# A spare tile of 160 bytes instead of 32 at the high end of SBUF: where the two halves of the buffers stand modulo 2048 bytes

## The chip, the cores and the metric

The kernel runs on one NeuronCore of one Trainium2 chip. The metric is the device time of one execution, in microseconds (us). Five engines work side by side and meet at semaphores: TensorE (PE; its weight loads are listed apart as PEld), VectorE (DVE), ScalarE (ACT), GpSimd (POOL), and SyncE (SP), which issues most of the DMA transfers. A matmul on PE has two operands in SBUF, the core's on-chip memory of 128 partitions: the stationary one (128 columns, loaded by a weight load just before) and the moving one (up to 512 columns, streamed through). The result goes to PSUM.

## The reference

One layer of an encoder on x of shape 1 x 1024 x 1024 in float32: a SwiGLU half step, a mixer of attention (4 query heads, 2 key heads of 128) and a bidirectional gated recurrence (4 heads of 128), a second SwiGLU half step with an inner width of 2816, and a last norm.

```
def swiglu_half_step(x, gain, w_in, w_out):
    h = rms_norm(x, gain)
    gate, up = jnp.split(h @ w_in, 2, axis=-1)
    return (jax.nn.silu(gate) * up) @ w_out
...
x = x + 0.5 * swiglu_half_step(x, ffn1_norm[l], ffn1_w_in[l], ffn1_w_out[l])
x = x + hybrid_mixer(x, l, ...)
x = x + 0.5 * swiglu_half_step(x, ffn2_norm[l], ffn2_w_in[l], ffn2_w_out[l])
x = rms_norm(x, final_norm[l])
```

## The kernel before

**Numbers.** Almost every product runs in three matmuls on operands that are split into a high and a low part (`split`, L103 and L104: ACT copies the high part, DVE subtracts it from the source). So one product of 128 rows is (high, high), (high, low), (low, high).

**Stages.** The kernel goes through five stages, each with pools of buffers of its own.

- `ffn_up`, for both half steps. The first two of the 22 column blocks are computed plainly (`plain`, L277, 256 columns at a time); the other 20 by a scheme of seven half-size products (`product`, L294, 512 columns). `unit` does seven `product` calls for one column block, and each is 4 blocks of k times 3 matmuls. The stationary operand is a weight tile from the pool `wop` (`hl_in_ffn`), the moving one a tile of the pools `B` or `T` (`ffn_B`, `ffn_T`).
- `ffn_down`, for both half steps: L402, 512 columns; stationary `hl_act_ffn` (pool `ah`), moving `hl_out_ffn` (pool `wo`).
- The mixer's projections: `proj_T` (L167, 512 columns; stationary `hl_rec_w`, moving `hm`) and `natural` (L495, 256 columns; stationary `hm`, moving the weights), and between them the recurrence.
- Attention: scores `s` (L798, 512 columns, stationary `qT`, moving `kT`), values `pv` (L830, 256 columns), and the output projection `project` (L855, 512 columns), which is called for the recurrence (`py`, stationary `recT`, moving `hl_wor`) and for the attention (`pa`, stationary `oT`, moving `hl_woa`).

The profile writes a matmul as out<-moving,stationary.

**Order.** The framework schedules the instructions when the program is built, and derives the waits from which tiles share memory. Loads stand in SP's queue in that order.

**Addresses.** A pool with `side="right"` takes its memory from the high end of SBUF downwards, the others from the low end upwards. All buffers named below are multiples of 2048 bytes apart within their side (small tiles of statistics and some of the recurrence are not), so each side has one residue modulo 2048. On the right the first tile is the spare one, `align` (L55), which no instruction reads or writes. The places in the built program, in bytes from the start of a partition:

| tiles | side | starts at | modulo 2048 |
|---|---|---|---|
| `hl_in_ffn` (wop) | left | 55104, then every 4096 | 1856 |
| `hl_out_ffn` (wo), `hl_act_ffn` (ah) | left | 44864 and 73536, then every 4096 | 1856 |
| `qT`, `recT` | left | 55104, 38720 | 1856 |
| `ffn_T`, `ffn_B` | right | 114624 and 163776, then every 16384 | 1984 |
| `hm`, `kT`, `v_attn`, `pT` | right | 163776, then every 16384 | 1984 |
| `hl_rec_w`, `hl_ri_w`, `hl_wor`, `hl_woa` (w2, the last of four in wo) | right | 139200, then every 8192; 90048 | 1984 |
| `oT` | right | 98240, 106432 | 1984 |

Inside a tile a matmul's operand starts at a multiple of 512 bytes, a moving one of 512 columns at a multiple of 2048. So a matmul has a relation of its own between its two operands: both left, both right, or one on each side, and in the last case the two starts differ by 128 bytes more than a multiple of 512. Both left: L402. Both right: L167, L495, L830 and `pa` of L855. One on each side: L277, L294, L798 and `py` of L855.

Of the kernel before, what the change touches and what calls it, by code (L numbers as in the profile page):

```python
# [12 lines left out]
F32 = mybir.dt.float32  # L13
# [8 lines left out]
P = 128  # L22
# [22 lines left out]
class Trunk:  # L45
    def __init__(self, ctx, tc, io):
        self.tc, self.nc, self.io = tc, tc.nc, io
        nc = self.nc
        pool = lambda name, **kw: ctx.enter_context(tc.tile_pool(name=name, **kw))
        self.const = pool("const", bufs=1)  # L50
        self.gpool = pool("gains", bufs=1)
        self.stat = pool("stat", bufs=4)
        self.dpool = pool("scratch", bufs=1, space=bass.MemoryType.DRAM)
        self.ident = self.const.tile([P, P], F32, name="ident")
        pool("align", bufs=1, side="right").tile([P, 8], F32, name="align")  # L55
        make_identity(nc, self.ident)
        self.banks = {}

# [1097 lines left out]
```

## Time and profile before

| what | us |
|---|---|
| median of 3 runs | 2138.0 (2133.77 to 2138.9) |
| the profiled execution | 2136.09 |
| its span, first to last instruction | 2134.3 |
| PE busy | 2053.5 (96%) |
| DVE, ACT, POOL busy | 1160.3, 780.2, 390.5 |

The profiled execution's own time stands 1.8 us above its span. Matmuls are pipelined: one is listed with about 390 ns, but the next starts long before its end. How fast they go is read from their number in a stretch in which PE doesn't stop, or from the starts of two groups. A list of a stretch counts every matmul that has any part in it.

### The profile page before, as it was taken

The page shows a single profiled execution, that of the slowest core. Times are in us where ns is not written, and L with a number is a line of the kernel's source. Part 1 is how long each engine was busy: PE and PEld are TensorE (multiplying, and loading weights), DVE is VectorE, ACT ScalarE, POOL GpSimd, SP SyncE. Part 2 cuts the span into 40 slices and gives each one's busy share as a digit, 9 for nine tenths or more (in the row PEclk, how much of TensorE's full clock was granted, in tenths as well). Part 3 has the DMA queues.
Part 4 walks back from the last instruction along what each step waited for, and adds up shares of the span by engine and source line. Part 5 has one row for each costly group of instructions (what it writes and reads, how often), then busy time and mean ns, then how long its engine had stood idle before and what let it go on. Part 6 is the DMA issues. An engine that isn't in the chain of part 4 may idle for free.

```text
span 2134.3 us, 27958 instructions
## 1 busy us (share of the span) xinstructions
PE 2053.5 (96%) x10849; PEld 1755.2 (82%) x10849; DVE 1160.3 (54%) x1951; ACT 780.2 (37%) x1295; POOL 390.5 (18%) x278
## 2 busy tenths in 40 slices
PE   5899999999999899999998999988999999999998
PEld 5888888887888798989998888878888888878886
DVE  6555554535363516788872567654645554443634
ACT  4333333324343313333332546533333333333432
POOL 2333232210000000121120323312422222100000
PEclk9999999999999999999999999999999999999999
DMA  5422322117464211121234522363322221264542
GB/s 167 124 80 80 93 89 74 60 70 260 142 223 148 74 45 43 32 80 40 80 100 148 175 92 81 108 192 105 98 84 79 75 89 55 74 236 142 185 148 79
DMA packets 208124, 232.12 MB, mean 109 GB/s; under 512 B 9444, under 2 KB 169464, under 8 KB 207992
## 3 DMA queue, kind: packets, MB, share of 16 engines
q1 hardware_dynamic: 205688, 221.95, 32.9%
q0 software_dynamic: 2304, 8.39, 1.0%
q8 instruction: 85, 1.39, 0.3%
q14 instruction: 47, 0.39, 0.1%
HBM read 175.78 MB, written 54.53 MB: 108 GB/s over the span
## 4 chain that ended last, share of the span: by engine, by line
PE 90%; DVE 5%; ACT 2%; DMA 1%; issue 1%; POOL 0%; SPq 0%; DVEq 0%; ACTq 0%; POOLq 0%
PE py_ffn L402 22%; PE pa_ffn L294 16%; PE pd_ffn L294 10%; PE rec_ps L167 6%; PE pc_ffn L294 5%; PE pb_ffn L294 5%; PE pp_ffn L277 4%; PE ri_ps L495 2%; PE rg_ps L495 2%; PE lv L561 2%; PE s L798 2%; PE py L855 2%; PE pv L830 2%; PE pa L855 2%; PE aq_ps L495 1%
## 5 line engine op out<-in xcount | busy, mean ns | idle before, releaser
L402 PE MATMUL py_ffn<-hl_out_ffn,hl_act_ffn 128*128 128x512 f32 x2112 | 482.4, 390 | 4.0 <-ACT hl_out_ffn L103 3.4
L402 PEld LDWEIGHTS py_ffn<-hl_out_ffn,hl_act_ffn 128*128 128x128 f32 x2112 | 397.0, 188 | 88.6 <-ACT hl_out_ffn L103 5.0
L104 DVE TENSOR_TENSOR hl_out_ffn<-raw_out_ffn,hl_out_ffn 128x512 fp32r<-128x512 f32 x176 | 120.1, 688 | 235.1 <-ACT hl_out_ffn L103 234.9
L294 PE MATMUL pa_ffn<-ffn_T,hl_in_ffn_S 128*128 128x512 f32 x960 | 242.4, 395 | 0.0
L294 PEld LDWEIGHTS pa_ffn<-ffn_T,hl_in_ffn_S 128*128 128x128 f32 x960 | 180.8, 188 | 42.1
L103 ACT CAST hl_out_ffn<-raw_out_ffn 128x512 fp32r<-128x512 f32 x176 | 107.8, 620 | 266.1 <-PE py_ffn L402 258.4
L104 DVE TENSOR_TENSOR hl_in_ffn_S<-s_ffn,hl_in_ffn_S 128x512 fp32r<-128x512 f32 x160 | 163.6, 1026 | 29.4 <-ACT hl_in_ffn_S L103 29.4
L103 ACT CAST hl_in_ffn_S<-s_ffn 128x512 fp32r<-128x512 f32 x160 | 99.1, 621 | 201.3 <-PE pd_ffn L294 175.2
L104 DVE TENSOR_TENSOR hl_in_ffn_A<-raw_in_ffn,hl_in_ffn_A 128x512 fp32r<-128x512 f32 x128 | 103.5, 813 | 125.7 <-ACT hl_in_ffn_A L103 125.7
L103 ACT CAST hl_in_ffn_A<-raw_in_ffn 128x512 fp32r<-128x512 f32 x136 | 83.7, 623 | 182.2 <-PE pc_ffn L294 77.8
L167 PE MATMUL rec_ps<-hm,hl_rec_w 128*128 128x512 f32 x576 | 134.7, 392 | 0.0
L167 PEld LDWEIGHTS rec_ps<-hm,hl_rec_w 128*128 128x128 f32 x576 | 107.1, 188 | 21.6
L294 PE MATMUL pd_ffn<-ffn_T,hl_in_ffn_S 128*128 128x512 f32 x480 | 124.6, 395 | 0.0
L294 PE MATMUL pb_ffn<-ffn_B,hl_in_ffn_A 128*128 128x512 f32 x480 | 124.2, 395 | 0.0
L294 PE MATMUL pa_ffn<-ffn_B,hl_in_ffn_A 128*128 128x512 f32 x480 | 119.4, 398 | 0.0
L294 PE MATMUL pc_ffn<-ffn_T,hl_in_ffn_A 128*128 128x512 f32 x480 | 118.0, 394 | 0.0
L294 PE MATMUL pd_ffn<-ffn_B,hl_in_ffn_S 128*128 128x512 f32 x456 | 112.1, 394 | 0.0
L294 PEld LDWEIGHTS pa_ffn<-ffn_B,hl_in_ffn_A 128*128 128x128 f32 x480 | 91.2, 191 | 21.1
L294 PEld LDWEIGHTS pb_ffn<-ffn_B,hl_in_ffn_A 128*128 128x128 f32 x480 | 90.5, 189 | 21.2
L294 PEld LDWEIGHTS pd_ffn<-ffn_T,hl_in_ffn_S 128*128 128x128 f32 x480 | 90.5, 188 | 21.2
L277 PE MATMUL pp_ffn<-ffn_B,hl_in_ffn_A 128*128 128x256 f32 x768 | 101.1, 294 | 6.9 <-DVE ffn_B L186 3.9
L294 PEld LDWEIGHTS pc_ffn<-ffn_T,hl_in_ffn_A 128*128 128x128 f32 x480 | 90.4, 188 | 21.1
(245 smaller groups left out, 3123.7 us busy)
## 6 DMA issues: line engine op xcount, KB each, us to landing
raw_in_ffn<-in_ffn_w_in SPq DMA_DIRECT2D x88, 512.0 KB, 4.2
raw_out_ffn<-in_ffn_w_out SPq DMA_DIRECT2D x88, 512.0 KB, 3.8
raw_act_ffn<-d_act SPq DMA_DIRECT2D x88, 256.0 KB, 4.0
d_act<-g_ffn SPq DMA_DIRECT2D x80, 256.0 KB, 2.2
x<-d_x SPq DMA_DIRECT2D x24, 512.0 KB, 4.9
x<-in_x SPq DMA_DIRECT2D x16, 512.0 KB, 5.3
d_x<-x SPq DMA_DIRECT2D x16, 512.0 KB, 2.8
raw_rec_w<-in_w_in_mix SPq DMA_DIRECT2D x12, 512.0 KB, 4.0
```

What stands on the lines that cost most here:

```text
L103: nc.scalar.copy(hl[:, 0, :], src)
L104: (lo_engine or nc.vector).tensor_sub(hl[:, 1, :], src, hl[:, 0, :].bitcast(F32))
L167: nc.tensor.matmul(out, hl[:, a, ks], h[half][b][:, k, cols], start=(k == 0 and i == 0), stop=(k == NK - 1 and i == 2),)
L277: nc.tensor.matmul(ps[j][:, odd * 256 : (odd + 1) * 256], A[2 * j + k // 4][:, a, ks], B[k // 4][:, b, k % 4, cols], start=(k == 0 and i = ...
L294: nc.tensor.matmul(ps, A[:, a, ks], T[key][:, b, k, :], start=(first and k == 0 and i == 0), stop=(k == 3 and i == 2), skip_group_check=True,)
L402: nc.tensor.matmul(py[d], ah[:, a, o : o + P], wo[d][:, b, :], start=(f == 0 and i == 0), stop=(f == NF - 1 and i == 2),)
L495: nc.tensor.matmul(ps[:, tt, :], h[half][a][:, k, ts], hl[k // 4][:, b, ws], start=(k == 0 and i == 0), stop=(k == NK - 1 and i == 2),)
L561: nc.tensor.matmul(pl[:, cs], now[:, 0, cs], now[:, 1, cs], start=True, stop=True)
L798: nc.tensor.matmul(ps[:, ks], qT[:, a, qs], kT[:, b, kv, ks], start=(i == 0), stop=(i == 2))
L830: nc.tensor.matmul(ps, vt[:, j, a, vs], pT[j][:, b, i4, :], start=(st == 0 and i == 0), stop=(st == NT - 1 and i == 2),)
L855: nc.tensor.matmul(py, lhs(a, n), units[n][:, b, ds], start=(n == 0 and i == 0), stop=(n == 3 and i == 2),)
```

## The change

```
-        pool("align", bufs=1, side="right").tile([P, 8], F32, name="align")
+        pool("align", bufs=1, side="right").tile([P, 40], F32, name="align")
```

The spare tile takes 40 floats instead of 8, so every buffer of the right side moves down by 128 bytes: residue 1856 in place of 1984. Nothing on the left moves. `ffn_T` then begins at 114496, the byte at which the topmost left buffer of that stage ends. The order of the instructions is the same on all five engines. What changes beside the addresses is two waits, one added and one moved, because other pieces of memory now overlap.

On POOL, at the start of the second half step's `ffn_up` (the sums of L221 to L223; `x_7` and `xn_` are the last rows of attention, being stored; in brackets stand the semaphores waited for, by engine or DMA queue; `t_ffn_0` are the sums of the first row pair):

```order
 L910 DMA d_xn_78<-xn_n_6_11700 128x1024 [waits DMASW5_49,DVE_49]
 L904 DMA d_x_77<-x_7_11715 128x1024 [waits DMAHW7_49,DMASW6_49,DVE_49]
-L223 TENSOR_TENSOR t_ffn_0_12108<-t_ffn_0_12106,xn_0_11801 128x512 [waits DMAHW4_49,DVE_49]
+L223 TENSOR_TENSOR t_ffn_0_12108<-t_ffn_0_12106,xn_0_11801 128x512 [waits DMAHW4_49,DVE_49,PE_49]
 L910 DMA d_xn_78<-xn_n_7_11746 128x1024 [waits DMASW7_49,DVE_49]
 L221 TENSOR_TENSOR t_ffn_1_12172<-xn_3_11839 128x512 [waits DMAHW0_49,PE_49,Pool_49]
```

The first sum that L223 makes there now waits for PE as well: for the last `pa` matmul of attention, since its buffer now overlaps the place of `oT`.

On SP, in the second half step's `ffn_down` (L1094 loads the rows of x; DMASW are the transfers that POOL issued, those of L904 among them):

```order
 L385 DMA raw_act_ffn_7_0_15659<-d_act_102 128x2x256 [waits DMAHW5_49,DVE_49]
 L1094 DMA x_0_15477<-d_x_77 128x1024 [waits Pool_49]
-L1094 DMA x_1_15479<-d_x_77 128x1024 [waits DMASW6_49,DMAHW6_49,DMASW4_49,PE_49]
-L1094 DMA x_2_15481<-d_x_77 128x1024 [waits DMAHW7_49]
+L1094 DMA x_1_15479<-d_x_77 128x1024 [waits DMAHW6_49,DMASW6_49,PE_49]
+L1094 DMA x_2_15481<-d_x_77 128x1024 [waits DMAHW7_49,DMASW4_49]
 L1094 DMA x_3_15483<-d_x_77 128x1024 [waits DMAHW2_49,DMAHW0_49]
 L383 DMA raw_out_ffn_7_0_15657<-in_ffn_w_out 128x1024 [waits DMAHW1_49,DVE_49]
```

One wait for a transfer of POOL's goes from the second load to the third.

## Rows read from the trace of the kernel before

**Rows 1.** The page: busy time of each engine (share of the span) and number of instructions; the chain of work that ended last, by engine and by line.

```profile
PE 2053.5 (96%) x10849; PEld 1755.2 (82%) x10849; DVE 1160.3 (54%) x1951; ACT 780.2 (37%) x1295; POOL 390.5 (18%) x278
...
PE 90%; DVE 5%; ACT 2%; DMA 1%; issue 1%; POOL 0%; SPq 0%; DVEq 0%; ACTq 0%; POOLq 0%
PE py_ffn L402 22%; PE pa_ffn L294 16%; PE pd_ffn L294 10%; PE rec_ps L167 6%; PE pc_ffn L294 5%; PE pb_ffn L294 5%; PE pp_ffn L277 4%; PE ri_ps L495 2%; PE rg_ps L495 2%; PE lv L561 2%; PE s L798 2%; PE py L855 2%; PE pv L830 2%; PE pa L855 2%; PE aq_ps L495 1%
```

**Rows 2.** Matmuls in three stretches that hold nothing but L294: stretch, its length, PE's busy time and number of matmuls, granted clock of PE, DMA share, GB/s.

```profile
100.00:280.00 180.00, 180.00 (x776) 1.00 0.29 85
290.00:480.00 190.00, 190.00 (x819) 1.00 0.22 71
1500.00:1870.00 370.00, 370.00 (x1594) 1.00 0.25 77
```

**Rows 3.** The same view for two stretches of L402 alone, and for two of L167 alone (the last two lines).

```profile
500.00:720.00 220.00, 220.00 (x972) 1.00 0.55 177
1890.00:2110.00 220.00, 220.00 (x972) 1.00 0.53 173
...
796.00:832.00 36.00, 36.00 (x160) 1.00 0.20 59
1026.00:1046.00 20.00, 20.00 (x90) 1.00 0.42 132
```

**Rows 4.** The instructions of single lines: number, shortest, median and longest duration in ns as the profile lists it, first and last start in us, shapes. L294, L402, L167, L855 and L798 in turn.

```profile
L294 PE MATMUL pa_ffn<-ffn_T,hl_in_ffn_S x960: 390/393/404, 107.3 to 1880.1; 128*128 128x512 f32 x192
...
L294 PE MATMUL pa_ffn<-ffn_B,hl_in_ffn_A x480: 390/392/776, 97.2 to 1857.8; 128*128 128x512 f32 x160
...
L294 PE MATMUL pb_ffn<-ffn_B,hl_in_ffn_A x480: 390/393/404, 100.5 to 1863.4; 128*128 128x512 f32 x160
...
L294 PE MATMUL pc_ffn<-ffn_T,hl_in_ffn_A x480: 390/393/404, 103.3 to 1866.1; 128*128 128x512 f32 x160
...
L294 PE MATMUL pd_ffn<-ffn_T,hl_in_ffn_S x480: 390/393/404, 106.1 to 1874.5; 128*128 128x512 f32 x160
...
L294 PE MATMUL pd_ffn<-ffn_B,hl_in_ffn_S x456: 390/392/404, 124.7 to 1870.8; 128*128 128x512 f32 x152
...
L294 PE MATMUL pe_ffn<-ffn_B,hl_in_ffn_S x24: 390/393/404, 482.9 to 1877.3; 128*128 128x512 f32 x24
...
L402 PE MATMUL py_ffn<-hl_out_ffn,hl_act_ffn x2112: 387/389/761, 490.4 to 2123.4; 128*128 128x512 f32 x192
...
L167 PE MATMUL rec_ps<-hm,hl_rec_w x576: 387/389/481, 794.6 to 1046.6; 128*128 128x512 f32 x192
...
L855 PE MATMUL py<-hl_wor,recT x192: 389/393/689, 1176.3 to 1262.0; 128*128 128x512 f32 x192
...
L855 PE MATMUL pa<-hl_woa,oT x192: 387/389/497, 1270.8 to 1407.8; 128*128 128x512 f32 x192
...
L798 PE MATMUL s<-kT,qT x192: 387/395/628, 1167.8 to 1372.4; 128*128 128x512 f32 x192
```

**Rows 5.** PE in order of time, in attention: start in us, time from the first start to the last end, engine, line, operation, tiles, shapes, number.

```profile
1244.16 5.75 PE L855 MATMUL py<-hl_wor,recT 128*128 128x512 f32 x24
1249.76 0.51 PE L830 MATMUL pv<-pT,v_attn 128*128 128x256 f32 x3
...
1330.32 2.99 PE L855 MATMUL pa<-hl_woa,oT 128*128 128x512 f32 x12
1333.14 0.60 PE L817 MATMUL ptp<-ident,p 128*128 128x128 f32 x4
...
1396.99 11.19 PE L855 MATMUL pa<-hl_woa,oT 128*128 128x512 f32 x48
```

**Rows 6.** The view of rows 2 for matmuls of 256 columns: a stretch of L277 and one of L495.

```profile
30.00:52.00 22.00, 22.00 (x188) 1.00 0.28 93
1104.00:1160.00 56.00, 56.00 (x469) 1.00 0.45 146
```

**Rows 7.** All engines in a stretch of `ffn_up` and in the two parts of attention (busy time and number for PE, PEld, DVE, ACT, POOL, then granted clock, DMA share, GB/s); and one group of L294 in the view by line (busy time, mean ns of one, idle time of PE before them).

```profile
290.00:480.00 190.00, 190.00 (x819) 154.03 (x819) 89.75 (x127) 64.57 (x112) 45.29 (x33) 1.00 0.22 71
...
1176.00:1262.00 86.00, 84.68 (x465) 71.66 (x464) 48.03 (x70) 39.73 (x69) 27.14 (x20) 1.00 0.43 145
1270.00:1408.00 138.00, 128.31 (x784) 111.42 (x783) 98.28 (x231) 77.90 (x145) 45.49 (x42) 1.00 0.33 107
...
L294 PE MATMUL pa_ffn<-ffn_T,hl_in_ffn_S 128*128 128x512 f32 x960 | 242.4, 395 | 0.0
```

**Rows 8.** The places of the two waits: POOL in order of time (start, duration, and in brackets the idle time before and who ended it); then L904 on POOL with its transfers' time to landing, and L1094 on SP's queue, in the view of rows 4.

```profile
1413.57 1.64 POOL L223 TENSOR_TENSOR t_ffn<-t_ffn,xn 128x512 f32<-128x512 f32 x1 [2.59 <-DVE t_ffn L222]
...
L904 POOL DMA_DIRECT2D d_x<-x x8: 533/604/762, 1281.1 to 1410.4; - x8
...
DMA to landing us min/median/max: 3.0/4.1/5.7
...
L1094 SPq DMA_DIRECT2D x<-d_x x8: 319/430/1242, 1893.6 to 1902.5; - x8
```

## The prediction

> **What bounds the kernel now.** I read the page first: busy times and the chain of work that ended last [rows 1]. PE is busy 96% of the span and makes up 90% of that chain, so a change that touches no instruction can only matter by how fast PE's matmuls follow each other. L294 and L402 are the two big lines of the chain: the four L294 entries together hold 36%, L402 holds 22%. Next I took stretches that hold one line only and counted matmuls [rows 2, 3]. A list counts every matmul with any part in the stretch, and one lasts some 0.39 us [rows 4], so the spacing is (length + 0.39 us) / number.
>
> - L294: 180.39 / 776, 190.39 / 819 and 370.39 / 1594 all give 232.4 ns [rows 2].
> - L402: 220.39 / 972 gives 226.7 ns, twice [rows 3].
> - L167: 36.39 / 160 and 20.39 / 90 give 227.4 and 226.6 ns [rows 3].
>
> All three are matmuls of 128 by 512 with 128 stationary columns, at a granted clock of 1.00, the 2.4 GHz level, with PE never idle in the stretch. L402 keeps its 226.7 with DMA at a share of 0.55, L294 is slower at 0.22 to 0.29, so transfers aren't the reason. What goes with the difference is the sides of the operands. L402 has both on the left, L167 both on the right, L294 one on each. L167's moving tile `hm` stands at the very addresses of `ffn_B`, and L402's stationary tiles have the residue of L294's, so it is neither operand alone.
>
> The durations say it again, and inside one stage [rows 4]. With both operands on one side (L402, L167, `pa`) shortest and median are 387 and 389 ns each time. With one on each side L294 has 390 and 392 or 393, `py` 389 and 393, `s` a median of 395. `py` and `pa` are the same line and the same loop, in the same stage; only the tiles differ. The spacings of attention agree: 24 `py` matmuls from 1244.16 to the next group at 1249.76 are 233.3 ns each; 48 `pa` matmuls, 11.19 us less one duration over 47, are 229.8 [rows 5].
>
> **The change, part by part.**
>
> *L294.* After it both operands have residue 1856, the relation that L402 has today. Its matmuls number 960 + 4 x 480 + 456 + 24 = 3360 [rows 4]. PE is idle for 0.0 us before them [rows 7], so their spacing is the stage's time. If it goes from 232.4 to 226.7, the gain is 5.7 ns x 3360 = 19.1 us. The trace has no matmul of L294 at equal residue, so I bound the new spacing: 226.6, the fastest row at equal residue, gives 19.5 us; 235, the slowest (12 `pa` matmuls from 1330.32 to 1333.14 [rows 5], between short pieces of other work), gives a loss of 8.7 us. I take 226.7, because L294 runs without a break as L402 does, which is the nearest row; that slow `pa` piece follows a switch of kind. What is late next: in the 190 us of [rows 7] DVE is busy for 89.75, ACT 64.57, POOL 45.29, at a DMA share of 0.22. PE needs 2.5% less time; none of them comes near.
>
> *`py` and `s`.* 192 each [rows 4], with one operand on each side. Their stretches are short, so I take from them not L402's spacing but what `pa` reaches: 233.3 - 229.8 = 3.5 ns x 384 = 1.3 us. PE is busy 84.68 of 86 us and 128.31 of 138 in these parts [rows 7], so most of it is on the path: 1.0 us. Bounds: 0, if the waits between pieces take it, and 384 x 6.6 ns (233.3 down to 226.7) = 2.5 us.
>
> *L277.* 256 columns, operands on both sides; the wide matmuls' penalty is not there. With 0.29 us for one, 22.29 / 188 = 118.6 ns against 56.29 / 469 = 120.0 for L495, whose operands have equal residue [rows 6]. If L277 takes L495's spacing, its 768 matmuls lose 1.1 us. It stands half beside waits for its operands early in both stages, so I count a loss of 0.5 us; bounds 0 and 1.1.
>
> *L830, L495, L167, `pa`, L402.* Both operands move together or neither does: nothing.
>
> *The two waits.* L223 now also waits for the last `pa` matmul. That ends at 1396.99 + 11.19 = 1408.18 [rows 5], L223 starts at 1413.57 after it waited for DVE [rows 8]: met 5.4 us earlier. Behind it in POOL's queue stand the last store of xn and L221, neither later than now. On SP, the transfers of L904 are issued by 1410.4 and land within 5.7 us, the loads of L1094 begin at 1893.6 [rows 8]: met by 480 us. Both cost nothing. The cover would be gone only if attention ended 5.4 us later against L223, and it doesn't.
>
> *The spare tile.* No instruction touches it: nothing.
>
> Sum: -19.1 - 1.0 + 0.5 = -19.6 us. The profiled execution took 2136.09, its span 2134.3; that gives 2116.5. The median of the runs, 2138.0, stands 1.9 us above the profiled one and the fastest run 2.3 below it. I split the difference and say 2117.
>
> **A rule that speaks against it.** L402 and L294 differ by 5.7 ns a matmul [rows 2, 3]. The Trainium skill, page "TensorE: Matmul & The Clock Gate", section "Part 2: What happens when you issue a matmul", says that TensorE reads the stationary and the moving operand through two independent ports, so that loading weights doesn't take bandwidth from a running matmul; "SBUF — State Buffer", section "SBUF: two separate sides", says that TensorE never waits for anyone there. By these two the addresses couldn't matter and the time would stay at 2136 to 2138. The trace doesn't agree: `py` and `pa` differ in nothing but where their tiles stand.
>
> **The rivals.**
>
> 1. *The residues aren't the cause, and nothing changes: 2137.* Then L294 would be slowed by what works beside it, such as POOL, busy 45.29 us there [rows 7] and not at all in `ffn_down`. Against it: POOL is busy in both parts of attention too, 27.14 of 86 us where `py` runs and 45.49 of 138 where `pa` runs [rows 7], and `pa` has the fast median. For it: no row shows a right and a left operand at equal residue. This holds the case that the distance, and not the residue, decides. The two rules above end here.
> 2. *Half the gain: 2126.* Equal residue lets the matmuls run fast only after some undisturbed ones, and in L294 the product, the moving tile and the PSUM bank change every 12. The spacing then stays at the 229.8 of the long `pa` piece: 2.6 x 3360 = 8.7 us, with the other terms at -0.5 some 9 us. For it: `pa` does have slow pieces. Against it: L167 begins a new output every 24 matmuls and stays at 226.6 to 227.4.
> 3. *Slower: 2145.* Stationary and moving operand, and the tiles that POOL, DVE and ACT write in `ffn_up`, all at one residue, meet more often than now, and L294 takes the 235 ns of the slow `pa` piece throughout: (235 - 232.4) x 3360 = 8.7 us more. This decides from a spacing over 232.4 + 6.4 / 3.36 = 234.3 on. For it: that piece had equal residues, and POOL, DVE and ACT were at work. Against it: L402 runs at 226.7 with DVE and ACT writing tiles of its own residue.
>
> **How the numbers follow.** My forecast 0.84, rival 1 0.06, rival 2 0.06, rival 3 0.04. About 0.3% (6.4 us) is what a measurement of this kernel tells from no change, so forecast and rival 2 count as faster: 0.90; rival 1 as the same: 0.06; rival 3 as slower: 0.04. The range: fast end 2136.09 - 19.5 - 2.5 = 2114, less the 2.3 by which the fastest run lay under the profiled one, and some for the estimate: 2110. Slow end: 2136.09 - 19.1 + 1.1 = 2118, plus the 2.8 by which the slowest run (2138.9) lay above it, is 2121, drawn towards rival 2 to 2125. That leaves out rivals 1 to 3 (0.16) and a little of the first case.
>
> **What would show it.** Right: a stretch of L294 alone counts 370.39 / 0.2267 = 1634 matmuls in 370 us instead of 1594, and the shortest and median durations of L294 become 387 and 389. `ffn_up` ends some 9.5 us earlier in each half step, L402 and L167 are as before, and the median of `py` and `s` falls towards 389. L277 at 120 ns would show its small loss; L223 waiting for PE would show the new wait to matter. Wrong: L294 still at 232, as rival 1 has it; at 230, rival 2; above 234, rival 3. A gain that appears in `ffn_down` or the projections would contradict the whole argument.

## The result and the profile after

The changed kernel takes a median of 2116.49 us (2113.86 to 2119.14, 4 runs) against 2138.45 before (2133.77 to 2141.13, 4 runs). The ratio is 0.9903, with a 95% interval of 0.9891 to 0.9916: 18 to 23 us faster. The forecast was 2117. All ratios and intervals here compare fast runs alone, which leaves out one execution of 5252.87 us in E3.

The page first, its line of busy times and the chain by engine:

```profile
PE 2032.2 (96%) x10849; PEld 1754.3 (83%) x10849; DVE 1166.2 (55%) x1951; ACT 780.3 (37%) x1295; POOL 392.5 (19%) x278
...
PE 90%; DVE 5%; DMA 2%; issue 1%; ACT 1%; POOL 0%; SPq 0%; DVEq 0%; ACTq 0%; POOLq 0%
```

Beside [rows 1], the same 10849 matmuls took 21.3 us less of PE's time, and the span went from 2134.3 to 2114.7, 19.6 us less. PE is still 90% of the chain: nothing else has become the bound.

Where PE got the time back shows in the stretches that hold one line only. Those of L294 (stretch, length, PE's busy time and matmuls, granted clock, DMA share, GB/s):

```profile
100.00:280.00 180.00, 180.00 (x796) 1.00 0.30 89
290.00:470.00 180.00, 180.00 (x796) 1.00 0.23 74
1500.00:1850.00 350.00, 350.00 (x1545) 1.00 0.26 79
```

The first stretch is the one of [rows 2] to the microsecond: 796 matmuls instead of 776. With the 0.39 us of one matmul added to the length, the spacing is 180.39 / 796 = 226.6, again 226.6, and 350.39 / 1545 = 226.8 ns, where it was 232.4. L402 hasn't moved, 210.39 / 928 = 226.7 and 200.39 / 885 = 226.4:

```profile
500.00:710.00 210.00, 210.00 (x928) 1.00 0.54 169
1890.00:2090.00 200.00, 200.00 (x885) 1.00 0.49 154
```

The durations of single lines (number, shortest, median, longest in ns, first and last start in us), to be read against [rows 4]:

```profile
L294 PE MATMUL pa_ffn<-ffn_T,hl_in_ffn_S x960: 388/390/390, 107.8 to 1861.4; 128*128 128x512 f32 x192
...
L294 PE MATMUL pd_ffn<-ffn_T,hl_in_ffn_S x480: 388/390/390, 106.7 to 1855.9; 128*128 128x512 f32 x160
...
L798 PE MATMUL s<-kT,qT x192: 387/394/629, 1159.8 to 1364.3; 128*128 128x512 f32 x192
...
L855 PE MATMUL py<-hl_wor,recT x192: 387/390/775, 1168.1 to 1253.0; 128*128 128x512 f32 x192
...
L855 PE MATMUL pa<-hl_woa,oT x192: 387/390/497, 1261.7 to 1400.6; 128*128 128x512 f32 x192
```

For these two groups of L294 the shortest, median and longest duration now lie within 2 ns, where they ran from 390 to 404. `py` has gone from 389 and 393 to 387 and 390, the values of `pa`.

The first starts of the lines cut the span into stages, and each stage's length is the difference of two of them. For the kernel before, after, and the two that make half of the change each:

| from the first start of | to | before | after | E1: `ffn_up` alone | E2: attention alone |
|---|---|---|---|---|---|
| L277, first half step | L294 | 67.3 | 68.3 | 68.5 | 69.2 |
| L294, first half step | L402 | 393.2 | 383.3 | 383.5 | 393.4 |
| L402, first half step | L495 `ri` | 256.8 | 256.8 | 256.8 | 257.6 |
| L495 `ri` | L798 | 420.6 | 421.5 | 421.5 | 422.7 |
| L798 | last start of L855 | 240.0 | 240.7 | 241.6 | 243.8 |
| last start of L855 | L277, second | 8.7 | 7.2 | 7.6 | 7.2 |
| L277, second half step | L294 | 72.5 | 72.7 | 72.1 | 72.3 |
| L294, second half step | L402 | 393.2 | 383.0 | 384.3 | 394.1 |
| L402, second half step | end of the span | 252.1 | 251.3 | 252.2 | 251.3 |

Two stages carry the gain, 9.9 and 10.2 us. The rest adds up to half a microsecond.

### The profile page after: what moved, and what is told of

It reads as the page before. It is cut to its first block, busy times and chain, and to the rows that moved or that the text cites. A ratio compares the mean times of both kernels' runs of the same rounds, so it can differ in the third digit from the quotient of the medians.

```text
span 2114.7 us, 27958 instructions
## 1 busy us (share of the span) xinstructions
PE 2032.2 (96%) x10849; PEld 1754.3 (83%) x10849; DVE 1166.2 (55%) x1951; ACT 780.3 (37%) x1295; POOL 392.5 (19%) x278
## 4 chain that ended last, share of the span: by engine, by line
PE 90%; DVE 5%; DMA 2%; issue 1%; ACT 1%; POOL 0%; SPq 0%; DVEq 0%; ACTq 0%; POOLq 0%
PE py_ffn L402 22%; PE pa_ffn L294 15%; PE pd_ffn L294 10%; PE rec_ps L167 6%; PE pc_ffn L294 5%; PE pb_ffn L294 5%; PE pp_ffn L277 5%; PE ri_ps L495 2%; PE rg_ps L495 2%; PE py L855 2%; PE lv L561 2%; PE s L798 2%; PE pv L830 2%; PE pa L855 1%; PE aq_ps L495 1%
## 5 line engine op out<-in xcount | busy, mean ns | idle before, releaser
L402 PE MATMUL py_ffn<-hl_out_ffn,hl_act_ffn 128*128 128x512 f32 x2112 | 481.0, 390 | 4.5 <-ACT hl_out_ffn L103 3.4
L402 PEld LDWEIGHTS py_ffn<-hl_out_ffn,hl_act_ffn 128*128 128x128 f32 x2112 | 396.3, 188 | 88.4 <-ACT hl_out_ffn L103 4.9
L294 PE MATMUL pa_ffn<-ffn_T,hl_in_ffn_S 128*128 128x512 f32 x960 | 236.8, 390 | 0.0
L294 PEld LDWEIGHTS pa_ffn<-ffn_T,hl_in_ffn_S 128*128 128x128 f32 x960 | 180.4, 188 | 37.2
L167 PE MATMUL rec_ps<-hm,hl_rec_w 128*128 128x512 f32 x576 | 135.9, 395 | 0.0
L167 PEld LDWEIGHTS rec_ps<-hm,hl_rec_w 128*128 128x128 f32 x576 | 108.1, 190 | 21.8
L294 PE MATMUL pd_ffn<-ffn_T,hl_in_ffn_S 128*128 128x512 f32 x480 | 121.8, 389 | 0.0
L294 PE MATMUL pb_ffn<-ffn_B,hl_in_ffn_A 128*128 128x512 f32 x480 | 121.5, 390 | 0.0
L294 PE MATMUL pa_ffn<-ffn_B,hl_in_ffn_A 128*128 128x512 f32 x480 | 116.0, 391 | 0.0
L294 PE MATMUL pc_ffn<-ffn_T,hl_in_ffn_A 128*128 128x512 f32 x480 | 115.3, 390 | 0.0
L294 PE MATMUL pd_ffn<-ffn_B,hl_in_ffn_S 128*128 128x512 f32 x456 | 109.5, 390 | 0.0
L277 PE MATMUL pp_ffn<-ffn_B,hl_in_ffn_A 128*128 128x256 f32 x768 | 100.2, 293 | 6.6 <-ACT xn_n L121 2.2
L294 PEld LDWEIGHTS pa_ffn<-ffn_B,hl_in_ffn_A 128*128 128x128 f32 x480 | 90.4, 189 | 18.5
L294 PEld LDWEIGHTS pb_ffn<-ffn_B,hl_in_ffn_A 128*128 128x128 f32 x480 | 90.2, 188 | 18.6
L294 PEld LDWEIGHTS pc_ffn<-ffn_T,hl_in_ffn_A 128*128 128x128 f32 x480 | 90.2, 188 | 18.6
L294 PEld LDWEIGHTS pd_ffn<-ffn_T,hl_in_ffn_S 128*128 128x128 f32 x480 | 90.2, 188 | 18.6
```

Source lines behind the costliest of these rows:

```text
L167: nc.tensor.matmul(out, hl[:, a, ks], h[half][b][:, k, cols], start=(k == 0 and i == 0), stop=(k == NK - 1 and i == 2),)
L277: nc.tensor.matmul(ps[j][:, odd * 256 : (odd + 1) * 256], A[2 * j + k // 4][:, a, ks], B[k // 4][:, b, k % 4, cols], start=(k == 0 and i = ...
L294: nc.tensor.matmul(ps, A[:, a, ks], T[key][:, b, k, :], start=(first and k == 0 and i == 0), stop=(k == 3 and i == 2), skip_group_check=True,)
L402: nc.tensor.matmul(py[d], ah[:, a, o : o + P], wo[d][:, b, :], start=(f == 0 and i == 0), stop=(f == NF - 1 and i == 2),)
```

## The experiments

All twelve compute the same with the same matmuls. Addresses differ, and with them, as in the change, a wait here and there; in E11 also the number of raw weight buffers and with it the order of some instructions.

**E1, only `ffn_up`.**

```
-                k.B, k.T = sbuf(up, "B", 4, side="right"), sbuf(up, "T", 3, side="right")
+                sbuf(up, "pad", 1, side="right").tile([P, 32], F32, name="pad"); k.B, k.T = sbuf(up, "B", 4, side="right"), sbuf(up, "T", 3, side="right")
```

> The spare tile stays at 32 bytes; 128 bytes are put ahead of the right-hand pools of ffn_up alone, so only L277 and L294 get operands of equal residue (1856); attention keeps 128 bytes of difference. Theory R (the relation of the two operands of a matmul decides): L294 goes from 232.4 to 226.7 ns a matmul in both half steps, py and s stay at medians of 393 and 395; 2136 - 19 = about 2117 to 2119. Rival W (the gain comes from the moved waits or from attention): at most 1 us of gain, about 2137.

Measured: 2118.68 us, ratio 0.9909 (0.9894 to 0.9923). Two stretches of L294, in the view of [rows 2]:

```profile
290.00:470.00 180.00, 180.00 (x796) 1.00 0.23 74
1500.00:1700.00 200.00, 200.00 (x884) 1.00 0.27 83
```

226.6 and 200.39 / 884 = 226.7 ns. The whole gain, within the intervals, comes from the operands of L277 and L294.

**E2, only attention and the projections.**

```
-                k.hpool = hstack.enter_context(
+                hstack.enter_context(tc.tile_pool(name="pad", bufs=1, side="right")).tile([P, 32], F32, name="pad"); k.hpool = hstack.enter_context(
```

> The other half alone: the 128 bytes are put ahead of hm, so hm, w2 and the right-hand buffers of attention move to 1856, and the tiles of both ffn_up stay at 1984. Theory R: L294 stays at 232.4, py and s fall to a median near 389; a gain of 0 to 2.5 us, 2135 to 2138, not to be told from no change by the times. Rival W: about 2117.

Measured: 2136.35 us, ratio 0.9985 (0.9971 to 0.9999), that is 0 to 6 us faster. L294 in the first and the second half step, and then the durations of `py`:

```profile
110.00:280.00 170.00, 170.00 (x733) 1.00 0.27 81
1500.00:1700.00 200.00, 200.00 (x859) 1.00 0.29 86
```

```profile
L855 PE MATMUL py<-hl_wor,recT x192: 387/389/775, 1181.6 to 1266.4; 128*128 128x512 f32 x192
```

L294 stays slow, at 170.39 / 733 = 232.5 ns and 200.39 / 859 = 233.3 ns, while `py` has the durations of equal residues. Attention took 243.8 us in the profiled execution (table above), but at a granted clock of 0.97 from its first to its last matmul, where the kernel before had 0.99, so that this one length says little about the addresses. Rival W has fallen with these two runs. The interval ends just short of 1: it holds the 1 us forecast for attention, and hardly tells it from zero.

**E3, the same difference put where there was none.** In the second half step's `ffn_down`, both operands of L402 on the left, 128 bytes between the two pools:

```
-                k.draw, k.ar, k.wo, k.ah = (
-                    sbuf(down, key, n) for key, n in (("draw", 3), ("ar", 3), ("wo", 7), ("ah", 4))
-                )
+                k.draw, k.ar, k.wo = (sbuf(down, key, n) for key, n in (("draw", 3), ("ar", 3), ("wo", 7)))
+                if name == "ffn2": sbuf(down, "pad", 1).tile([P, 32], F32, name="pad")
+                k.ah = sbuf(down, "ah", 4)
```

> The kernel before with a pad of 128 bytes between the pools wo and ah of the second ffn_down alone: both operands of L402 are on the left there, but now 128 bytes apart modulo 512. Theory R: L402 goes from 226.7 to 232.4 ns in the second half step and stays at 226.7 in the first; 1056 x 5.7 = 6.0 us slower, about 2143 to 2144. Rival S (it is the two ends of SBUF, or what works beside L294, not the residue): nothing changes, 2138.

Measured: ratio 1.0037 (1.0025 to 1.0050), 5 to 11 us slower. L402 in the first and in the second half step:

```profile
500.00:720.00 220.00, 220.00 (x972) 1.00 0.55 182
1900.00:2100.00 200.00, 200.00 (x863) 1.00 0.54 180
```

220.39 / 972 = 226.7 ns where nothing was touched, 200.39 / 863 = 232.2 where the pad is. The starts of single matmuls in the trace go further: L402 there follows itself after 230, 233, 241, 232, 231, 232, 228, 230, 232, 241 ns, and L294 of the kernel before from 303.3 us on after 228, 230, 233, 240, 233, 231, 231, 229, 230, 232, 241, the same rhythm. L402 of the kernel before steps at 226, 227, 227. So neither the two ends of SBUF nor POOL, idle in `ffn_down`, makes the difference: 128 bytes between the operands do.

**E4, another residue for both.** A tile of 64 bytes at the low end, a spare tile of 96 at the high end:

```
-        self.ident = self.const.tile([P, P], F32, name="ident")
-        pool("align", bufs=1, side="right").tile([P, 8], F32, name="align")
+        self.const.tile([P, 16], F32, name="lpad"); self.ident = self.const.tile([P, P], F32, name="ident")
+        pool("align", bufs=1, side="right").tile([P, 24], F32, name="align")
```

> Both sides at residue 1920: 64 bytes of pad on the left, a spare tile of 96 bytes on the right. Theory R (relation): as the changed kernel, L294 at 226.7, about 2117. Rival A (the residue 1856 itself is the good one): L294 at 232 and, since L402 and L167 leave or never had 1856, perhaps L402 slower too; 2137 or more.

Measured: 2117.55 us, ratio 0.9891 (0.9871 to 0.9911). L294 and L402:

```profile
290.00:470.00 180.00, 180.00 (x796) 1.00 0.23 74
...
1890.00:2090.00 200.00, 200.00 (x884) 1.00 0.48 157
```

226.6 and 226.7 ns. The residue itself doesn't matter, only that the two agree. Rival A has fallen.

**E5 to E7, smaller differences.** The spare tile with 64, 96 and 128 bytes, so that the sides are 96, 64 and 32 bytes apart:

```
-        pool("align", bufs=1, side="right").tile([P, 8], F32, name="align")
+        pool("align", bufs=1, side="right").tile([P, 16], F32, name="align")
```

(24 and 32 in place of 16 in the other two.)

> Spare tile of 64 bytes: right side at 1952, 96 bytes from the left's 1856. Theory R1 (any difference costs the same): L294 at 232.4, about 2137. Rival R2 (the cost grows with the difference): 5.7 x 96 / 128 = 4.3 ns over 226.7, L294 at 231.0, about 2132.

> Spare tile of 96 bytes: right side at 1920, 64 bytes from the left's 1856. Theory R1 (any difference costs the same): L294 at 232.4, about 2137. Rival R2 (cost in proportion): L294 at 229.6, about 2127. Rival R3 (a difference of a multiple of 64 is as good as none): 226.7, about 2117; but then 128 should have been good too.

> Spare tile of 128 bytes: right side at 1888, 32 bytes from the left's 1856. Theory R1 (any difference costs the same): L294 at 232.4, about 2137. Rival R2 (cost in proportion): L294 at 228.1, about 2122. Rival R4 (operands within one small line meet as if equal): 226.7, about 2117.

Measured: 96 bytes, ratio 1.0025 (1.0015 to 1.0035); 64 bytes, 0.9940 (0.9916 to 0.9964); 32 bytes, 1.0017 (1.0007 to 1.0027). L294 with 96 bytes:

```profile
1500.00:1700.00 200.00, 200.00 (x859) 1.00 0.28 84
```

With 32 bytes:

```profile
1500.00:1700.00 200.00, 200.00 (x859) 1.00 0.28 85
```

And with 64 bytes, in both half steps:

```profile
110.00:280.00 170.00, 170.00 (x745) 1.00 0.28 85
290.00:470.00 180.00, 180.00 (x788) 1.00 0.23 74
1500.00:1700.00 200.00, 200.00 (x859) 1.00 0.28 84
1700.00:1840.00 140.00, 140.00 (x602) 1.00 0.19 61
```

32 and 96 bytes give 233.3 ns. That is about one more than most stretches at 128 bytes, and what the second half step of E2 had at 128; theory R1 was right that they cost, and a little low. The cost doesn't grow with the difference: R2 and R4 have fallen. At 64 bytes the first half step runs at 170.39 / 745 = 228.7 and 228.9 ns and the second at 200.39 / 859 = 233.3 and 233.2, in one execution, with the same instructions and the same addresses. None of the theories had said that. E2 shows a smaller step of the kind at 128 bytes, 232.5 and 233.3 ns in one execution. The runs of the kernel with 64 bytes spread from 2118.95 to 2132.11 us, as they would if executions differ in where the one and the other spacing holds; this is not shown, since only one of them was profiled, the slowest.

**E8 to E10 and E12, how equal is equal.** The pad of E3 with 256, 512, 64 and 192 bytes, one execution each; single times say nothing about a few microseconds, so only the spacing is read.

```
-                if name == "ffn2": sbuf(down, "pad", 1).tile([P, 32], F32, name="pad")
+                if name == "ffn2": sbuf(down, "pad", 1).tile([P, 64], F32, name="pad")
```

(128, 16 and 48 in place of 64 in the others; the diff is against E3.)

> As the run with 128 bytes between wo and ah in the second ffn_down, but with 256 bytes. Inside the tiles, differences of 512, 1024 and 1536 bytes already run at 226.7 ns. Theory R512 (equal means equal modulo 512): L402 of the second half step above 230 ns. Rival R256 (equal modulo 256 is enough): 226.7 ns.

> The same with 512 bytes: a control for the pad itself. Theory R512: 226.7 ns in both half steps, the time of the kernel before. Rival P (a pad between the pools slows L402 for another reason): about 232 ns in the second half step.

> The same with 64 bytes. With a spare tile of 96 bytes (64 bytes of difference) L294 stood at 229 ns in some stretches and 233 in others. If that belongs to the difference of 64 bytes, L402 of the second half step shows one or both of these spacings; if it belongs to ffn_up, it shows one of its own.

> As the runs with 64, 128 and 256 bytes between wo and ah in the second ffn_down, with 192 bytes. Theory R256: slow like 64 and 128, L402 of the second half step at 229 to 234 ns, 226.7 in the first.

L402 of the first and second half step with 256 bytes:

```profile
500.00:720.00 220.00, 220.00 (x972) 1.00 0.54 178
1900.00:2100.00 200.00, 200.00 (x884) 1.00 0.54 174
```

With 512 bytes, the second:

```profile
1900.00:2100.00 200.00, 200.00 (x884) 1.00 0.56 184
```

With 64 bytes:

```profile
500.00:720.00 220.00, 220.00 (x972) 1.00 0.56 182
1900.00:2100.00 200.00, 200.00 (x859) 1.00 0.54 173
```

With 192 bytes:

```profile
500.00:720.00 220.00, 220.00 (x972) 1.00 0.55 179
1900.00:2100.00 200.00, 200.00 (x876) 1.00 0.53 169
```

256 and 512 bytes: 200.39 / 884 = 226.7 ns, as if there were no pad. 64 bytes: 233.3; 192 bytes: 200.39 / 876 = 228.8. So theory R512 has fallen, and equality modulo 256 is enough for L402. The pads of 64 and 192 bytes show, in `ffn_down`, the two spacings that E6 showed in `ffn_up`, and in the starts of single matmuls the same rhythms: 233, 233, 234 ns with 64 bytes and in E6's second half step, 226, 229, 232 with 192 bytes and, within 1 ns, in E6's first.

**E11, 256 bytes in `ffn_up`.** B and T at 1600 against 1856 on the left:

```
-                sbuf(up, "pad", 1, side="right").tile([P, 32], F32, name="pad"); k.B, k.T = sbuf(up, "B", 4, side="right"), sbuf(up, "T", 3, side="right")
+                sbuf(up, "pad", 1, side="right").tile([P, 96], F32, name="pad"); k.B, k.T = sbuf(up, "B", 4, side="right"), sbuf(up, "T", 3, side="right")
...
-                    for key, n in (("raw", 7), ("wop", 9), ("s", 4), ("n", 3), ("c", 4))
+                    for key, n in (("raw", 6), ("wop", 9), ("s", 4), ("n", 3), ("c", 4))
```

(Against E1.)

> The spare tile at 32 bytes, 384 bytes ahead of the right-hand pools of ffn_up (B and T at 1600, that is 256 bytes from the left's 1856), and six raw weight buffers instead of seven there to make room, which changes the order of some transfers. Theory R256 (equal modulo 256 is enough, as in the second ffn_down with 256 bytes): L294 at 226.7 ns, 2117 to 2122 as with equal residues in ffn_up alone. Rival (L294 needs more than L402, equality modulo 2048): L294 at 230 or more, about 2135.

Measured: 2120.31 us, ratio 0.9917 (0.9892 to 0.9942). Two stretches of L294:

```profile
290.00:470.00 180.00, 180.00 (x796) 1.00 0.24 76
1500.00:1700.00 200.00, 200.00 (x884) 1.00 0.27 83
```

226.6 and 226.7 ns at residues that differ by 256 modulo 2048. The agreement modulo 2048 that the change is named for is more than is needed; it does the work because it contains agreement modulo 256.

## Why the prediction was right, point by point

- **L294, -19.1 us.** 5.7 ns x 3360 held: 232.4 became 226.6 to 226.8. The two stages shrank by 9.9 and 10.2, together 20.1 us, one more than the term. E1 shows that this alone makes the gain, E3 that the same 5.7 ns can be put on other matmuls at will. The choice of L402's row for the new spacing, and not the slow `pa` piece, was right; L294 runs like L402. The shortest and median durations came out at 388 and 390, where 387 and 389 were forecast, and L167 is much as it was, 34.39 / 152 = 226.3 ns against 227.4:

```profile
788.00:822.00 34.00, 34.00 (x152) 1.00 0.21 60
```

- **`py` and `s`, -1.0 us.** The first half of the term, that these matmuls get faster, held. The durations show it for `py`, in the change and in E2; for `s` they hardly do (median 395 before, 394 after). The starts of single matmuls show it for both: the mean step from one to the next, where they follow each other without a break, went from 232.6 to 227.9 ns for `py` and from 232.5 to 229.9 for `s`, that is 0.9 and 0.5 us over 192 of each. From the first to the last start of `py` it is 85.7 us before and 84.9 after, 84.9 and 84.8 in E4 and E2, where its operands agree as well, and 85.0 to 86.0 in the seven other kernels that leave them 128 bytes off. The second half, that most of it comes out in the time, is not shown: the stage from the first `s` to the last `pa` was 240.0 us before and 240.7 after. What else differs is the granted clock. The part of `pa`, whose operands agree before and after, went from 137.0 to 138.9 us between its first and last start. [rows 7] has a granted clock of 1.00 there, the second line here 0.98:

```profile
1168.00:1254.00 86.00, 84.73 (x469) 72.59 (x467) 48.18 (x71) 40.70 (x70) 28.14 (x21) 0.99 0.43 147
1262.00:1400.00 138.00, 128.78 (x772) 112.58 (x771) 96.82 (x227) 77.19 (x143) 46.80 (x43) 0.98 0.32 107
```

  After the change PE ran there for some 3 us at a time at 0.50, the 1.2 GHz level, twice, each time after a few microseconds in which it had stood idle for about a third (the view of [rows 2]; the microseconds ahead of each spell, then the spell):

```profile
1330.00:1337.00 7.00, 4.95 (x34) 1.00 0.40 133
...
1338.00:1341.00 3.00, 3.00 (x10) 0.50 0.67 261
...
1375.00:1381.00 6.00, 4.06 (x35) 1.00 0.76 288
...
1382.00:1385.00 3.00, 3.00 (x15) 0.50 0.20 49
```

  Over the fourteen kernels of this study, most with the same attention, the stage took 239.1 to 240.0 us where its granted clock was 0.99, 239.9 to 241.6 at 0.98 and 241.6 to 244.6 at 0.97 and 0.96. A gain of 1 us in it, or a loss, can't be read from its length.
- **L277, +0.5 us.** In the view of [rows 6], L277 and then L495:

```profile
30.00:52.00 22.00, 22.00 (x184) 1.00 0.30 94
1097.00:1151.00 54.00, 54.00 (x452) 1.00 0.46 147
```

  22.29 / 184 = 121.1 ns, against 118.6 before and 120.1 for L495: matmuls of 256 columns gained nothing. The loss is not shown to come from the addresses. The same stretch of the first half step, with 188 matmuls before, holds 178 to 186 in the six kernels that leave `ffn_up` as it was (E2, E3, E8 to E10, E12) and 180 to 185 in the four whose operands agree modulo 256 there (the change, E1, E4, E11). In E12:

```profile
30.00:52.00 22.00, 22.00 (x181) 1.00 0.29 91
```

  The stages that hold L277 grew by 1.0 and 0.2 us, which includes waits for operands.
- **The two waits, 0.** The end of `pa` and the start of L223 on POOL:

```profile
1389.79 11.17 PE L855 MATMUL pa<-hl_woa,oT 128*128 128x512 f32 x48
```

```profile
1405.98 2.20 POOL L223 TENSOR_TENSOR t_ffn<-t_ffn,xn 128x512 f32<-128x512 f32 x1 [2.92 <-PE pt_ffn_B L182]
```

  L223 starts 5.0 us after the last `pa` ends at 1400.96; before it was 5.4. The bracket names PE for a transpose (`pt_ffn_B`) that ended late, not for the `pa` that the new wait is for and that had long ended. The piece from the last `pa` to L277 is 7.2 us, 1.5 less than before.
- **The sum.** -19.6 us by the terms, -19.6 by the span. That they agree to a tenth is partly luck: the two stages of L294 gave 1.0 more than their term, and all the others together grew by 0.5, where the terms had them shrink by 0.5.
- **The rivals.** 1 (nothing changes) and 3 (slower) are out by the result. 2 (half the gain) is out by the spacing of 226.6: the change of product every 12 matmuls doesn't hold L294 back. Rival 1's cause, what works beside L294, is out by E3 with its control E9. What the prediction drew from its two rules of the Trainium skill, that the addresses couldn't matter, doesn't hold for these matmuls; the measurement decides.

What stays open is why. The runs show which distances between the operands cost, not which part of the chip makes them cost. They also don't tell what chooses between 229 and 233 ns at a distance of 64 bytes, or between 232.4 and 233.3 at 128.

## What to carry to other kernels

A matmul's spacing can depend on where its two operands stand relative to each other. Here 512 columns of fp32r (the type in which the profile lists the split operands) took 226.7 ns when the starts agreed modulo 256 bytes and 229 to 233 when they were 32, 64, 96, 128 or 192 bytes off, while 256 columns showed no such cost. Where PE is the bound, compare the counts per stretch of lines of one shape, and where they differ look at the addresses. The durations are only a hint: in E3 `py` stands 128 bytes off, as before, and yet has the shortest duration of equal residues:

```profile
L855 PE MATMUL py<-hl_wor,recT x192: 387/393/777, 1181.4 to 1266.9; 128*128 128x512 f32 x192
```

A spare tile of a few bytes, between pools or at one end of memory, was the whole remedy. Expect to see it in the time only where PE runs without a break: attention's matmuls got faster too, but the length of their stage, which moved by up to 5.5 us from one profiled execution to the next, doesn't show it.

## What was not expected of the hardware

- A smaller distance need not cost less: 32 and 96 bytes gave 233.3 ns, 128 gave 232.4 in most stretches and 233.3 in others (E2).
- At a distance of 64 bytes the same instructions at the same addresses ran at 228.7 ns in the first half step and at 233.3 in the second (E6). At 128 bytes E2 has 232.5 in the first and 233.3 in the second. So the distance alone doesn't set the spacing.
- Agreement modulo 256 is enough, for operands on one side (E8) and on two (E11).
